# Two-layer decoder trunk on one core: a shorter run of plain units behind a block of seven products, and scratch transfers begun by GpSimd

## The chip, the cores and the metric

The kernel runs on one core of a Trainium2 chip. The metric is the device time of one execution in microseconds. Before the change it is 2709.37 us, the median of 3 runs (2709.22 to 2713.18).

TensorE multiplies matrices and writes its sums to PSUM; VectorE, ScalarE and GpSimd work on tiles in SBUF (the first two in PSUM too); SyncE begins DMA transfers. Each engine takes its instructions in the order in which the program gives them, and waits for the others by semaphores.

## The reference, cut to what matters

Two layers work on a residual stream `x` of 256 tokens by 2048 features, all in float32:

```python
for i in range(2):
    h = rms_norm(x, mix_norm[i])
    y = stick_breaking_mixer(h, ...) if i == 0 else gated_deltanet_mixer(h, ...)
    x = x + y
    x = x + (silu(g) * u) @ w_down[i]     # g, u = split(rms_norm(x, ffn_norm[i]) @ w_gu[i])
```

The first mixer projects to q, k and v (2048 x 6144), normalises q and k per head, takes q k^T for 16 heads of 128, weights each past key by a stick-breaking product, multiplies with v and projects out (2048 x 2048). The second is a gated DeltaNet (GDN) with a 2048 x 12352 input projection, a short convolution, a chunked recurrence and a 4096 x 2048 output projection. Each FFN has a hidden width of 5632: `w_gu` is 2048 x 11264 and `w_down` 5632 x 2048.

## The kernel before, in words

**Units.** All weights go through the core once. A *block* is a product of the 256 tokens with 512 columns of a weight; it is cut into *units* of 256 rows of it (512 KB). A unit is loaded by SyncE (`load`, L519), split by ScalarE into a rounded high part (L328) and by VectorE into the low rest (L332) (`convert`), and multiplied by TensorE (`product`, L354): high by high, high by low and low by high. A plain unit is 12 matmuls of 512 columns.

**Blocks of seven products.** In each FFN the gate and up columns of the hidden parts 0, 2, 4, 6, 8 and 10 (`SEVEN`), 12 blocks in all, are computed by a scheme of the Strassen kind: 7 products of half-size blocks in place of 8, 21 matmuls of 256 columns to a unit. It needs sums of the weights' quarters (`sums`, on VectorE, three instructions) and of the operands'. A block has eight units. At its end `quarters` reads out the four PSUM banks with one ScalarE and four VectorE instructions, and the next such block may begin only then. Seven-product units have two buffers of converted weights ("w" in the rows), plain units among them two others ("slabs").

**The order.** In an FFN, ten plain units in the ordinary lane come first, then a part in which seven-product and plain units are mixed, then plain ones. `merge` (L1026) chooses the mix by a search over all orders with a list of penalties: 4 for each plain unit short of two behind a finished block, 1 more where there are just two, 0.3 for two seven-product units in a row (three are not allowed), 2 for more than three plain ones in a row, and 0.15 for each unit by which the plain ones depart by more than 1.5 from 1.3 (`RATIO`) per seven-product unit. Of equal orders the one found first stays.

**The planner.** The kernel writes its instructions in an order that a small clock model in Python sets. Blocks' ends, norms and attention heads are tasks (generators); `stream` goes through the units, converts up to three units ahead (`AHEAD`), gives a unit's products and lets tasks run between them (`tick`). A task that has yielded goes on when the model's time for its last instructions has passed. A transfer's end is modelled by `transfer`; `later` and `nap` add pauses before a task's next step. The model only sets the order; on the chip the semaphores hold.

**Scratch transfers.** Some 128 x 1024 tiles are transposed by way of DRAM: VectorE transposes 32 x 32 pieces in place (L897 and L939), four writes of 32 partitions put them in place in a scratch tile (`way`, 128 KB each in runs of 128 bytes), and two reads bring them back in runs of 512 bytes (256 KB each). `turn` (L891) does this for q and k of the attention layer (8 sets) and for six parts of the norms' inputs; `turned_pairs` (L933) does it for the FFN's hidden activations (11 sets to each FFN), which it then splits into high and low operands ("kh", "kl") for the down projection. All these transfers are begun by SyncE at L367, in one queue with the weight loads. `turn` and `turned_pairs` pause before the first write (`TURN`, `WAY`) and between writes (`STEP`, `NAP`). GpSimd only fills tiles with constants, in the GDN layer above all.

Of the kernel before, what the change touches and what calls it, by code (L numbers as in the profile page):

```python
# [15 lines left out]
P = 128  # L16
D = 2048
S = 256
NT = S // P
# [12 lines left out]
class Slots:  # L32
# [37 lines left out]
    def put(self, *items):  # L70
        self.free.extend(items)
# [86 lines left out]
class Trunk:  # L158
# [20 lines left out]
    CONST = 14.0  # L179
    EARLY = 6  # L180
    LATER = 1.5
    WAY, NAP = 3.0, 1.2
    TURN, STEP = 1.0, 1.2
    TURNED = ((1, 0), (1, 1), (2, 0), (2, 1), (3, 0), (3, 1))
    GDN_ORDER = [('qk', 0), ('ba',), ('v', 0), ('qk', 1), ('z', 0), ('v', 2), ('v', 1), ('z', 1), ('qk', 2), ('qk', 3), ('v', 3), ('z', 2), ('z', 3), ('out', 0, 4), ('out', 4, 8), ('qk', 4), ('v', 4), ('qk', 5), ('v', 5), ('z', 5), ('z', 4), ('qk', 7), ('v', 6), ('qk', 6), ('out', 8, 16), ('v', 7), ('z', 6), ('z', 7), ('out', 16, 24), ('out', 24, 32)]

# [179 lines left out]
    def dma(self, out, in_):  # L366
        self.nc.sync.dma_start(out, in_)  # L367
        n = 4
        for d in out.shape:
            n *= d  # L370
        self.cur.ends("dma", self.transfer(n * (2 if out.shape[-1] * 4 <= 512 else 1), self.cur.begins("dma")))

    def transfer(self, nbytes, ready):
        issue = max(self.t["sp"], ready, self.t["pe"])
        self.t["sp"] = issue + 0.46
        self.t["dma"] = max(self.t["dma"], issue + 1.55) + nbytes / 3.6e5
        return self.t["dma"] + 0.55
# [367 lines left out]
    def norm_part(self, st, n):  # L745

        turned = (st.k, n) in self.TURNED
        if turned:
            parts = yield from self.two()
            yield from self.turn(parts, src=[self.x[t][n] for t in range(NT)])  # L750
        for half in range(2):
            if turned:
                src, put = parts[half], self.slabs.put
            else:
                src, put = (yield from self.banks.get()), self.banks.put
            bv = src.rearrange("p (k s) -> p k s", k=2)
            if not turned:
                for j in range(2):
                    kk = half * 2 + j
                    for t in range(NT):  # L760
                        self.tr(bv[:, j, t * P:(t + 1) * P], self.x[t][n][:, kk * P:(kk + 1) * P])
                yield
            kts = [n * 4 + half * 2 + j for j in range(2)]
            ops = [st.ops[kt] for kt in kts]
            gains = [self.gains[:, st.gain0 + kt:st.gain0 + kt + 1] for kt in kts]
            for j, o in enumerate(ops):
                self.act(o.hi, bv[:, j, :], scale=gains[j])
            for j, o in enumerate(ops):
                self.stt(o.lo, bv[:, j, :], gains[j], o.hi.bitcast(F32), ALU.mult, ALU.subtract)
                o.ready = True  # L770
            if st.forms is None:
                put(src)
            else:
                task = self.spawn(self.form_sums(st, n * 2 + half, src, put), f"forms {n} {half}")
                task.ready = self.t["pe"] + 2.0
        task = self.spawn(self.norm_stats(st, n), f"stats {n}")
        task.ready = self.t["pe"] + self.REST
# [110 lines left out]
        b = yield from self.slabs.get()  # L888
        return [a, b]

    def turn(self, parts, back=False, src=None):  # L891

        way = yield from self.ways.get()
        for i, s in enumerate(parts):
            self.nc.vector.transpose(s, src[i] if src else s)  # L897
            self.spend("dve", 0.07 + 0.00104 * NB)
            self.weave()
        self.cur.later = self.TURN  # L900
        yield
        flat = way[:]
        both = parts[0].tensor is parts[1].tensor and parts[1].offset - parts[0].offset == NB
        apart = not back and not both

        rows = (flat.rearrange("(c t) j -> c (t j)", t=2) if apart else flat).rearrange("(b i) j -> i b j", i=32)
        k = 0
        for a in range(4):
            m = slice(32 * a, 32 * a + 32)
            for n in range(1 if both else 2):  # L910
                if both:
                    dst, at = rows[:, :, m], self.joined(parts[0], 2)[m, :]
                elif back:
                    dst, at = rows[:, 16 * n:16 * n + 16, m], parts[n][m, :]
                else:
                    dst, at = rows[:, :, n * P + 32 * a:n * P + 32 * a + 32], parts[n][m, :]
                self.dma(dst, at.rearrange("p (b j) -> p b j", j=32))
                k += 1
            self.cur.nap = self.STEP if a < 3 else None
            yield  # L920
        for n in range(2):
            if back:
                self.dma(parts[n].rearrange("p (k c) -> p k c", k=4), flat.rearrange("(k t p) c -> t p k c", t=NT, p=P)[n])
            elif apart:
                self.dma(parts[n].rearrange("p (k c) -> p k c", k=2),
                         flat.rearrange("(c t) j -> c (t j)", t=2)[S * n:S * n + S, :].rearrange("(k p) c -> p k c", p=P))
            else:
                self.dma(self.joined(parts[0], 2).rearrange("p (k s) -> p k s", k=4)[:, :, n * P:(n + 1) * P],
                         flat[n * NB:(n + 1) * NB, :].rearrange("(k p) s -> p k s", p=P))
        yield  # L930
        self.ways.put(way)

    def turned_pairs(self, tok, stage, ops, put):  # L933

        way = yield from self.ways.get()
        for s, t in zip(self.cut(stage, NB), self.cut(tok, NB)):
            self.nc.vector.transpose(s, t)  # L939
            self.spend("dve", 0.07 + 0.00104 * NB)  # L940
            self.weave()
        self.cur.later = self.WAY
        yield

        rows = way[:].rearrange("(b i) j -> i b j", i=32)
        for a in range(4):
            m = slice(32 * a, 32 * a + 32)
            self.dma(rows[:, :, m], stage[m, :].rearrange("p (b j) -> p b j", j=32))
            self.cur.nap = self.NAP if a < 3 else None
            yield  # L950
        for t in range(NT):
            self.dma(tok.rearrange("p (k s) -> p k s", k=4)[:, :, t * P:(t + 1) * P],
                     way[t * NB:(t + 1) * NB, :].rearrange("(k p) s -> p k s", p=P))
            self.cur.nap = self.NAP if t < NT - 1 else None
            yield
        self.ways.put(way)
        if stage is not tok:
            self.duos.put(stage)
        for n, l in enumerate(self.cut(tok, NB)):
            pair = yield from self.pairs.get()  # L960
            self.operands_of(ops[2 * n:2 * n + 2], pair, l.rearrange("p (k s) -> p k s", k=2))
        put()


    def ffn_units(self, layer, norm, nxt, last, before, ahead=0):
# [52 lines left out]
        for b, n in zip(mids, turn):  # L1018
            b.sets = (n,)
# [6 lines left out]
    def merge(self, s, o):  # L1026


        ns, no = len(s), len(o)
        ends = [u.last for u in s]  # L1030
        best = {(0, 0, 0, 1, 3): (0.0, None)}
        layer = best
        trail = []
        for _ in range(ns + no):
            nextl = {}
            for st, (cost, _p) in layer.items():
                i, j, kind, run, gs = st

                for k in (0, 1):
                    ii, jj = i + k, j + 1 - k  # L1040
                    if ii > ns or jj > no or (k and kind == 1 and run >= 2):
                        continue
                    c = cost
                    if k:
                        c += 4.0 * max(0, 2 - gs) + (1.0 if gs == 2 else 0)
                        c += 0.3 * (kind == 1)
                        g2 = 0 if ends[i] else 3
                    else:
                        g2 = min(3, gs + 1)
                    r = min(run + 1, 4) if k == kind else 1  # L1050
                    if not k and r > 3 and ii < ns:
                        c += 2.0
                    if ii < ns:
                        c += 0.15 * max(0.0, abs(jj - self.RATIO * ii) - 1.5)
                    key = (ii, jj, k, r, g2)
                    if key not in nextl or nextl[key][0] > c:
                        nextl[key] = (c, st)
            trail.append(nextl)
            layer = nextl
        st = min(layer, key=lambda q: layer[q][0])  # L1060
        order = []
        for nextl in reversed(trail):
            order.append(st[2])
            st = nextl[st][1]
        return order[::-1]
# [727 lines left out]
```

## Time and profile before

| what | value |
|---|---|
| median of 3 runs | 2709.37 us |
| profiled execution | 2705.98 us |
| its span, first to last instruction | 2704.3 us |
| TensorE busy | 2669.4 us (99%) |
| VectorE busy | 2182.7 us (81%) |
| ScalarE busy | 1491.8 us (55%) |
| GpSimd busy | 11.2 us |
| granted TensorE clock | 1.0 |
| scratch writes, reads | 144, 72 |

In the profile PE is TensorE's matmuls, PEld its weight loads, DVE VectorE, ACT ScalarE, POOL GpSimd and SP SyncE; "SPq" means that SyncE's queue is meant. A row of the timeline has the start in us from the span's start, the length in us, the engine, the line of the kernel, the operation, the tiles written and read, how often, and in brackets the engine's idle time before it with what ended it. A row of the waits has who waited for whom, the total in us, how often, and the longest. Matmuls overlap, so the length of one (0.39 us for 512 columns) is more than the distance to the next (0.227 us).

### The profile page before, as it was taken

The numbers are of one execution on the slowest core, as the hardware profiler recorded it, in microseconds if no ns is written. First come the engines' busy times: TensorE is split into PE (matmuls) and PEld (weight loads), VectorE is DVE, ScalarE is ACT, GpSimd is POOL, SyncE is SP. The second block draws the span as 40 slices with busy tenths as digits, with TensorE's granted clock in tenths as the row PEclk, the third lists the DMA queues.
The fourth block names the chain that finished last, engine by engine and source line by source line (L and its number), as shares of the span: only waits on it lengthen the run. The fifth ranks groups of instructions, "written<-read, shape, count | busy, mean of one in ns | idle before, by whom it ended". The sixth has DMA issues, their size and how long they took to land.

```text
span 2704.3 us, 39527 instructions
## 1 busy us (share of the span) xinstructions
PE 2669.4 (99%) x14730; PEld 2274.6 (84%) x14730; DVE 2182.7 (81%) x3451; ACT 1491.8 (55%) x1961; POOL 11.2 (0%) x95
## 2 busy tenths in 40 slices
PE   9999999999999999999999999999999999999999
PEld 7888888888888888888888888888878888888887
DVE  6556568899999897678778887887679899989885
ACT  6555556554555554565665556645575555555453
POOL 0000000000000000000000000000000000000000
PEclk9999999999999999999999999999999999999999
DMA  7766775787676777855656556556567767767776
GB/s 245 202 185 196 219 211 164 208 231 212 203 218 205 208 211 233 227 174 172 182 143 195 159 161 175 168 153 186 170 191 212 223 196 220 217 188 218 226 209 188
DMA packets 487611, 534.41 MB, mean 198 GB/s; under 512 B 188087, under 2 KB 267258, under 8 KB 487418
## 3 DMA queue, kind: packets, MB, share of 16 engines
q1 hardware_dynamic: 487370, 531.87, 67.1%
q8 instruction: 115, 1.88, 0.3%
q14 instruction: 78, 0.64, 0.1%
q10 hardware_dynamic: 48, 0.02, 0.0%
HBM read 508.20 MB, written 23.59 MB: 197 GB/s over the span
## 4 chain that ended last, share of the span: by engine, by line
PE 83%; DVE 10%; issue 2%; ACT 2%; DMA 2%; SPq 0%; ACTq 0%; DVEq 0%
PE acc L354 61%; PE bank L354 20%; DVE w L332 5%; DVE slabs L332 2%; PE bank L363 1%; DMA slab<-in_ffn_w_gu_dram 1%; ACT slabs L328 1%; ACT w L328 1%; DVE slab L338 1%; DVE slab L332 1%; DVE slab L939 1%; DMA slab<-in_ffn_w_down_dram 0%; ACT slab L328 0%; DVE x L332 0%; DMA w<-in_ffn_w_gu_dram 0%
## 5 line engine op out<-in xcount | busy, mean ns | idle before, releaser
L332 DVE TENSOR_TENSOR w<-w,w 128x1024 fp32r<-128x1024 f32 (+2 forms) x746 | 946.3, 1285 | 249.0 <-ACT w L328 247.6
L328 ACT ACTIVATE w<-w 128x1024 fp32r<-128x1024 f32 (+2 forms) x650 | 802.8, 1244 | 417.8 <-PE acc L354 347.0
L354 PE MATMUL acc<-w,hTh 128*128 128x512 f32 (+1 forms) x3232 | 925.0, 369 | 9.1 <-DVE w L332 8.4
L354 PEld LDWEIGHTS acc<-w,hTh 128*128 128x128 f32 x3232 | 585.9, 189 | 120.5 <-DVE w L332 14.5
L354 PE MATMUL acc<-w,hTl 128*128 128x512 f32 (+1 forms) x1616 | 590.2, 365 | 3.1 <-DVE hTl L338 3.1
L328 ACT ACTIVATE slabs<-slab 128x1024 fp32r<-128x1024 f32 x264 | 279.3, 1058 | 431.9 <-DMA slab<-in_ffn_w_gu_dram 123.8
L332 DVE TENSOR_TENSOR slabs<-slab,slabs 128x1024 fp32r<-128x1024 f32 x264 | 321.5, 1218 | 93.1 <-ACT slabs L328 93.1
L354 PE MATMUL acc<-w,kh 128*128 128x512 f32 x1184 | 369.6, 393 | 0.0
L354 PEld LDWEIGHTS acc<-w,hTl 128*128 128x128 f32 x1616 | 304.5, 188 | 53.5 <-DVE hTl L338 3.9
L332 DVE TENSOR_TENSOR w<-w 128x256 f32<-128x256 f32 (+1 forms) x576 | 291.2, 508 | 9.8 <-DMA w<-in_ffn_w_gu_dram 2.6
L354 PEld LDWEIGHTS acc<-w,kh 128*128 128x128 f32 x1184 | 218.8, 188 | 43.7
L354 PE MATMUL acc<-w,kl 128*128 128x512 f32 x592 | 230.7, 390 | 0.0
L354 PE MATMUL acc<-slabs,hTh 128*128 128x512 f32 x608 | 190.1, 392 | 2.8 <-DVE slabs L332 2.8
L354 PE MATMUL bank<-w,wide 128*128 128x256 f32 x1296 | 178.9, 283 | 0.0
L354 PEld LDWEIGHTS bank<-w,wide 128*128 128x128 f32 x1296 | 165.8, 192 | 0.0
L354 PE MATMUL bank<-slabs,hTh 128*128 128x512 f32 x512 | 159.9, 392 | 3.1 <-DVE slabs L332 3.1
L354 PE MATMUL bank<-slabs,kh 128*128 128x512 f32 x512 | 159.6, 392 | 3.4 <-DVE slabs L332 3.4
L354 PE MATMUL acc<-slabs,kh 128*128 128x512 f32 x480 | 149.9, 392 | 2.1 <-DVE slabs L332 1.9
L354 PEld LDWEIGHTS acc<-slabs,hTh 128*128 128x128 f32 x608 | 111.0, 188 | 25.1 <-DVE slabs L332 4.9
L354 PEld LDWEIGHTS acc<-w,kl 128*128 128x128 f32 x592 | 111.1, 188 | 23.4
L354 PE MATMUL acc<-slabs,hTl 128*128 128x512 f32 x304 | 118.3, 389 | 0.0
L328 ACT ACTIVATE slab<-bank 32x128 f32<-32x128 f32 (+4 forms) x181 | 67.9, 379 | 89.3 <-PE bank L354 87.1
(216 smaller groups left out, 2933.4 us busy)
## 6 DMA issues: line engine op xcount, KB each, us to landing
w<-in_ffn_w_gu_dram SPq DMA_DIRECT2D x212, 512.0 KB, 4.5
slab<-in_ffn_w_gu_dram SPq DMA_DIRECT2D x140, 512.0 KB, 4.5
w<-in_gdn_w_in_dram SPq DMA_DIRECT2D x129, 512.0 KB, 4.3
slab<-in_ffn_w_down_dram SPq DMA_DIRECT2D x124, 512.0 KB, 4.5
w<-in_sb_w_in_dram SPq DMA_DIRECT2D x96, 512.0 KB, 4.5
w<-in_gdn_w_in_dram SPq DMA_DIRECT2D x128, 256.0 KB, 3.7
w<-in_gdn_w_out_dram SPq DMA_DIRECT2D x64, 512.0 KB, 4.4
w<-in_ffn_w_down_dram SPq DMA_DIRECT2D x52, 512.0 KB, 5.5
```

The lines of the kernel that those rows point to most:

```text
L328: self.nc.scalar.activation(out, in_, func, **kw)
L332: self.nc.vector.tensor_tensor(out, a, b, op=op)
L338: self.nc.vector.scalar_tensor_tensor(out, a, s, b, op0=op0, op1=op1)
L354: self.nc.tensor.matmul(out, lhsT, rhs, start=start, stop=stop, skip_group_check=True)
L363: self.nc.tensor.transpose(out, in_, self.ident[:p, :p])
L939: self.nc.vector.transpose(s, t)
```

## The change

The penalty of 1 for just two plain units behind a block of seven products is dropped. The scratch transfers of `turned_pairs`, and of `turn` for q and k, are begun by GpSimd through a new function `way_dma`; those of the norms stay with SyncE, with the pauses that they had (`LATE`, `NEXT`). In the model a transfer begun by GpSimd takes 6.5 us from its beginning (`OWN`), and takes no time of SyncE's queue or of the modelled DMA; the pauses before and between them are shorter.

```diff
-    WAY, NAP = 3.0, 1.2
-    TURN, STEP = 1.0, 1.2
+    WAY, NAP = 0.5, 0.8
+    TURN, STEP = 0.3, 0.8
+    OWN = 6.5
+    LATE, NEXT = 1.0, 1.2
...
+    def way_dma(self, out, in_):
+
+        self.nc.gpsimd.dma_start(out, in_)
+        self.cur.ends("dma", max(self.cur.begins("dma"), self.t["pe"]) + self.OWN)
...
-            yield from self.turn(parts, src=[self.x[t][n] for t in range(NT)])
+            yield from self.turn(parts, src=[self.x[t][n] for t in range(NT)], sp=True)
...
-    def turn(self, parts, back=False, src=None):
+    def turn(self, parts, back=False, src=None, sp=False):
...
         way = yield from self.ways.get()
+        move = self.dma if sp else self.way_dma
...
-        self.cur.later = self.TURN
+        self.cur.later = self.LATE if sp else self.TURN
...
-                self.dma(dst, at.rearrange("p (b j) -> p b j", j=32))
+                move(dst, at.rearrange("p (b j) -> p b j", j=32))
                 k += 1
-            self.cur.nap = self.STEP if a < 3 else None
+            self.cur.nap = (self.NEXT if sp else self.STEP) if a < 3 else None
...
-                self.dma(self.joined(parts[0], 2).rearrange("p (k s) -> p k s", k=4)[:, :, n * P:(n + 1) * P],
+                move(self.joined(parts[0], 2).rearrange("p (k s) -> p k s", k=4)[:, :, n * P:(n + 1) * P],
...
-            self.dma(rows[:, :, m], stage[m, :].rearrange("p (b j) -> p b j", j=32))
+            self.way_dma(rows[:, :, m], stage[m, :].rearrange("p (b j) -> p b j", j=32))
...
-            self.dma(tok.rearrange("p (k s) -> p k s", k=4)[:, :, t * P:(t + 1) * P],
+            self.way_dma(tok.rearrange("p (k s) -> p k s", k=4)[:, :, t * P:(t + 1) * P],
...
-                        c += 4.0 * max(0, 2 - gs) + (1.0 if gs == 2 else 0)
+                        c += 4.0 * max(0, 2 - gs)
```

More of the change, by code (lines that the diff above doesn't have):

```diff
@@ L922, in turn @@
             if back:
-                self.dma(parts[n].rearrange("p (k c) -> p k c", k=4), flat.rearrange("(k t p) c -> t p k c", t=NT, p=P)[n])
+                move(parts[n].rearrange("p (k c) -> p k c", k=4), flat.rearrange("(k t p) c -> t p k c", t=NT, p=P)[n])
             elif apart:
-                self.dma(parts[n].rearrange("p (k c) -> p k c", k=2),
+                move(parts[n].rearrange("p (k c) -> p k c", k=2),
                          flat.rearrange("(c t) j -> c (t j)", t=2)[S * n:S * n + S, :].rearrange("(k p) c -> p k c", p=P))
             else:
-                self.dma(self.joined(parts[0], 2).rearrange("p (k s) -> p k s", k=4)[:, :, n * P:(n + 1) * P],
+                move(self.joined(parts[0], 2).rearrange("p (k s) -> p k s", k=4)[:, :, n * P:(n + 1) * P],
                          flat[n * NB:(n + 1) * NB, :].rearrange("(k p) s -> p k s", p=P))
```

## The prediction

> **What bounds the kernel now.** I read the page's busy shares and its chain of waits first, then the stage table, then TensorE's waits.
>
> ```profile
> PE 2669.4 (99%) x14730; PEld 2274.6 (84%) x14730; DVE 2182.7 (81%) x3451; ACT 1491.8 (55%) x1961; POOL 11.2 (0%) x95
> PE 83%; DVE 10%; issue 2%; ACT 2%; DMA 2%; SPq 0%; ACTq 0%; DVEq 0%
> ```
>
> TensorE sets the time; its work isn't changed. All that a change of order can win is its idle time, 2704.3 - 2669.4 = 34.9 us. The stage table (start and length of the stretch, then PE, PEld, DVE, ACT busy) shows where that lies.
>
> ```profile
> 0.00:405.00 405.00, 398.16 (x1813) 330.25 (x1814) 244.10 (x317) 225.61 (x332) 2.70 (x14) 1.00 0.72 210
> 485.00:1040.00 555.00, 546.98 (x3261) 485.45 (x3260) 505.73 (x641) 292.79 (x255) 0.00 (x0) 1.00 0.72 211
> 2066.00:2620.00 554.00, 545.36 (x3248) 483.60 (x3248) 504.68 (x639) 292.69 (x255) 0.00 (x0) 1.00 0.72 210
> ```
>
> The first stretch is the attention layer, whose idle 6.8 us are nearly all start-up. The other two are the mixed parts of the FFNs, where units of seven products alternate with plain ones: 555.0 - 547.0 = 8.0 and 554.0 - 545.4 = 8.6 us idle, with VectorE at 91%. TensorE's waits say for whom:
>
> ```profile
> PE acc L354 <- DVE w L332: 8.4, 16, 1.0
> PE bank L354 <- DVE slabs L332: 6.5, 5, 1.6
> PE acc L354 <- DVE slabs L332: 4.7, 9, 0.9
> ```
>
> So it waits for converted weights: "slabs" are those of plain units, "w" those of seven-product units and of the unmixed stretches. It never waits for a weight transfer there; VectorE comes last. The timeline of one block end, on TensorE and then VectorE:
>
> ```profile
> 533.85 0.63 PE L354 MATMUL bank<-slabs,hTh 128*128 128x512 f32 x2
> ...
> 541.28 0.50 PE L354 MATMUL bank<-slabs,hTh 128*128 128x512 f32 x1 [1.57 <-DVE slabs L332]
> ```
>
> ```profile
> 532.63 1.23 DVE L332 TENSOR_TENSOR slabs<-slab,slabs 128x1024 fp32r<-128x1024 f32 x1 [3.15 <-ACT slabs L328]
> ...
> 538.83 1.29 DVE L939 STREAM_TRANSPOSE slab<-slab 128x512 f32<-128x512 f32 x2
> 540.04 1.18 DVE L332 TENSOR_TENSOR slabs<-slab,slabs 128x1024 fp32r<-128x1024 f32 x1
> 541.15 2.01 DVE L332 TENSOR_TENSOR w<-w,w 128x1792 fp32r<-128x1792 f32 x1
> ```
>
> The seven-product block ends at 533.85; three plain units follow, 2.72 us each (533.85, 536.6, 539.3 as they start). The wait of 1.57 us stands just inside the third. Plain units in the mix have two buffers of converted weights, so the third can't be converted before the first has run; by then VectorE is busy with reading out the ended block, and the third's conversion (540.04) stands behind that and behind the transposes. Before, VectorE had idled 3.15 us.
>
> **The change, the order of units.** The planner's list now takes two plain units behind a block at no penalty. Counting by hand: a block has eight seven-product units, seven gaps between them, and the list wants 1.3 x 8 = 10.4 plain units to a block. With three at the end, 7 + 3 = 10 fit and every second block has one double inside. With two and three equally cheap, ties go to the list that puts plain units early (they are tried first and a later equal one doesn't replace), so doubles go inside, one or two to a block, and two stay at the end. Units and products are the same in number.
>
> Removed: the waits in the third unit. Over both FFNs they are
>
> ```profile
> 491.89 0.50 PE L354 MATMUL acc<-slabs,hTh 128*128 128x512 f32 x1 [0.33 <-DVE slabs L332]
> 693.25 0.50 PE L354 MATMUL bank<-slabs,kh 128*128 128x512 f32 x1 [1.57 <-DVE slabs L332]
> 2072.48 0.50 PE L354 MATMUL acc<-slabs,hTh 128*128 128x512 f32 x1 [0.68 <-DVE slabs L332]
> 2121.87 0.50 PE L354 MATMUL bank<-slabs,hTh 128*128 128x512 f32 x1 [1.57 <-DVE slabs L332]
> 2172.92 0.50 PE L354 MATMUL bank<-slabs,kh 128*128 128x512 f32 x1 [0.23 <-DVE slabs L332]
> 2274.38 0.50 PE L354 MATMUL bank<-slabs,kh 128*128 128x512 f32 x1 [1.57 <-DVE slabs L332]
> ```
>
> With 541.28: 0.33 + 1.57 + 1.57 + 0.68 + 1.57 + 0.23 + 1.57 = 7.5 us, 45% of the two stages' 16.6.
>
> Added: the next block's first seven-product unit comes one plain unit earlier, with less cover. A block end without a wait shows its slack:
>
> ```profile
> 590.41 1.21 DVE L332 TENSOR_TENSOR slabs<-slab,slabs 128x1024 fp32r<-128x1024 f32 x1
> 591.88 2.02 DVE L332 TENSOR_TENSOR w<-w,w 128x1792 fp32r<-128x1792 f32 x1 [0.27 <-ACT w L328]
> 593.82 1.28 DVE L332 TENSOR_TENSOR x<-acc,x 128x512 f32<-128x512 f32 x2
> ```
>
> ```profile
> 586.25 0.63 PE L354 MATMUL acc<-slabs,kh 128*128 128x512 f32 x2
> ...
> 594.43 0.40 PE L354 MATMUL acc<-w,hTh 128*128 128x256 f32 x2
> ```
>
> The block ends at 586.25, the conversion at 593.82, the unit starts at 594.43: 0.6 us to spare. With two, it is due at 586.25 + 2 x 2.72 = 591.7. If the conversion stays where it is in VectorE's order, it loses only the third plain unit's 1.2 us and ends at 592.6: 0.9 us late. But the loop converts up to three units ahead before it lets the ended block's task run, so the conversion now goes ahead of the read-out, into time like the 3.15 us above, and the read-out has until 591.7. So a block end costs between 0 and 0.9 us; there are 2 x 11 with a block behind them, 0 to 20 us. I take 0.1, near the low end since the order of the loop decides it: +2.
>
> **The change, the scratch transfers.** 120 writes and 60 reads move from SyncE's queue to GpSimd's (of the 144 and 72 below, the norms' six sets of 4 and 2 stay).
>
> ```profile
> way<-slab SPq DMA_DIRECT2D x144, 128.0 KB, 5.3
> slab<-way SPq DMA_DIRECT2D x72, 256.0 KB, 5.0
> SPq L367 <- DMA way<-slab: 19.5, 12, 4.2
> ACT kh L328 <- DMA slab<-way: 25.2, 14, 5.0
> ```
>
> SyncE no longer stands 19.5 us in reads that wait for their writes, with weight loads behind. That is worth little: no TensorE wait in the mixed stages is ended by a transfer; an earlier load can only shorten VectorE's lateness behind it. I take -1, between 0 and a tenth of those 19.5, -2, since TensorE idles only 16.6 of the two stages' 1109 us. ScalarE's 25.2 us of waiting for landed reads holds up conversions behind it, but no TensorE wait follows from it: 0 now. The planner counts a set as landed 17.0 us after it begins (0.5 + 3 x 0.8 + 6.65 + 0.8 + 6.65) where it counted about 14.5, so the operands' conversions are placed later and ScalarE should wait less, also off the path. GpSimd itself is free (11.2 us busy); its reads now stand before the next set's writes, which nothing else queues behind until the GDN layer's fills.
>
> What no row shows is how long GpSimd takes to begin a write of 1024 runs of 128 bytes. The nearest is SyncE's own, in the tightest place, a k projection of the attention layer:
>
> ```profile
> 65.64 1.30 DVE L897 STREAM_TRANSPOSE slab<-slab 128x512 f32<-128x512 f32 x2
> 68.49 0.46 SPq L367 DMA_DIRECT2D way<-slab  x1
> 69.63 3.00 SPq L367 DMA_DIRECT2D way<-slab  x2
> 78.94 0.92 SPq L367 DMA_DIRECT2D slab<-way  x2
> DMA to landing us min/median/max: 3.9/4.4/4.9
> 84.94 0.81 PE L354 MATMUL bank<-slab 128*128 128x256 f32 x4
> ```
>
> The third of these writes holds SyncE 2.5 us, so a run of them goes at 1.2 to 1.5 us each. Transposed by 66.9, landed by about 83.5, used at 84.94, when the v projection's products are over: 1.4 us to spare. On GpSimd, with G us to begin a write and half of that a read (half as many runs), the k operand lands at 66.9 + 4G + 4.4 + G + 4.4, about 75.7 + 5G. Up to G = 1.8 nothing is late; above that TensorE stands 5 us for each us of G, in each of four head groups. Bounds: G = 0.46 (a lone issue) to 3.0 (SyncE's longest stretch for two), so 0 to 6 us x 4 = 24. I take G below 1.8 and 0, as SyncE's sustained rate is the nearest row.
>
> By the Trainium skill's DMA: Bandwidth & Descriptors, section Anatomy of one DMA — SWDGE (gpsimd) path, a transfer begun by GpSimd takes about 2.0 us and its bytes at 436 GB/s, 2.3 us for these writes, and many descriptors add little: an estimate by which k lands well before 84.94 and this term is 0. No run here shows it.
>
> **Sum.** 2705.98 (profiled execution; span 2704.3) - 7.5 + 2 - 1 = 2699.5. The median shown is 2709.37, 3.4 above that execution, so 2702.9; I say 2703.
>
> **Rivals.**
>
> First, the wait only changes place: the first seven-product unit, or the conversions behind it, take back what the third plain unit loses. VectorE's 91% speaks for it; the 3.15 us of idle VectorE ahead of the block end speaks against. Then -7.5 + 7 - 1: about 2708, no change.
>
> Second, two plain units are too few at every end: conversion behind read-out, 22 x 0.9 = 20 us: 2709.4 - 7.5 + 20 - 1 = 2721. It decides from 0.35 us an end. For it stands the 0.6 us of slack at 594.43; against it the loop's order.
>
> Third, GpSimd begins these writes slowly. At G = 3 each head group waits 75.7 + 15 - 84.9 = 5.8 us, 23 in all: 2703 + 23 = 2726; at G = 4, 2746. It decides from G = 2.1. For it: no such transfer is in the trace, and runs of 128 bytes already hold SyncE. A cause could be VectorE itself:
>
> ```profile
> L332 DVE TENSOR_TENSOR slabs<-slab,slabs 128x1024 fp32r<-128x1024 f32 x264 | 321.5, 1218 | 93.1 <-ACT slabs L328 93.1
> L897 DVE STREAM_TRANSPOSE slab<-slab 128x512 f32<-128x512 f32 x16 | 10.4, 687 | 0.0
> ```
>
> If VectorE held GpSimd off while it works, the sets would wait for its gaps, 161 us in the first 405; but these run at 1218 / 1024 = 1.19 and 687 / 512 = 1.34 ns an element, so none goes at a doubled rate. The Trainium skill's SBUF — State Buffer, section SBUF: two separate sides, warns against this very move: GpSimd can't write descriptors while VectorE runs in a two-port mode. By that rule the 1.19 ns rows are not such a mode and the trap stays open only for a handful of copies; no run here shows the lock.
>
> Fourth, the change does more than its terms: a better-filled VectorE clears most of the 16.6 us, 2709.4 - 14 = 2695. The other 16.6 - 7.5 = 9.1 us aren't behind a block's end, where the order gives way, so it has little.
>
> **How the numbers follow.** This measurement can tell about 0.2%, 5.4 us, from no change. My forecast (2703, own range 2699 to 2704) 0.36 and the fourth 0.07 make faster 0.43. The first, 0.28, is within. The second, 0.15, and the third, 0.14, are slower: 0.29. The range 2694 to 2727 leaves out most of the third above and a little of the fourth below.
>
> **What would show it.** Right: no TensorE wait two units behind a block's end, two plain units there; the idle time of the mixed stages at about 13 us together, not 16.6; ScalarE's wait for landed reads under 25 us; scratch writes on GpSimd about 1.5 us apart; the k operand landed before 84.9. Wrong: "PE <- DVE w" well above 8.4 us (second rival), TensorE waits for scratch reads in the attention layer (third), or the third unit's waits back at doubles inside a block (first).

## The result, and the profile after

| | before | after |
|---|---|---|
| median | 2709.4 us | 2692.4 us |
| profiled execution | 2705.98 us | 2691.59 us |
| its span | 2704.3 us | 2689.9 us |

The changed kernel takes 0.9935 of the time of the one before, interval 0.992 to 0.995: 17 us less, where 6 were forecast, and just below the forecast's range of 2694 to 2727. Of the 17, 14.4 lie between the two profiled executions; the remaining 2.6 come from how each of these stands to its own median.

First the page's busy shares and the chain of waits of the kernel after:

```profile
PE 2665.0 (99%) x14730; PEld 2275.6 (85%) x14730; DVE 2186.8 (81%) x3451; ACT 1488.5 (55%) x1961; POOL 150.8 (6%) x275
PE 84%; DVE 11%; DMA 2%; issue 2%; ACT 2%; DVEq 0%; ACTq 0%
```

The chain is TensorE's as before (84% after 83%). Its idle time went from 34.9 to 24.9 us, its busy time from 2669.4 to 2665.0 with the same 14730 matmuls. I take the 4.4 us of "busy" for waits too: matmuls overlap, so a wait between two of them partly disappears in the modelled length of the one before. Below, waits are therefore also measured from start to start: the distance from one matmul's start to the next, less what this distance usually is for the shape (the 20th percentile of the same execution), counted from 0.1 us on.

The stretches that the prediction used (start and length, then PE, PEld, DVE, ACT busy) are now

```profile
0.00:405.00 405.00, 398.28 (x1819) 330.97 (x1820) 245.02 (x321) 226.09 (x336) 40.02 (x62) 1.00 0.68 211
485.00:1040.00 555.00, 551.00 (x3279) 489.97 (x3278) 510.34 (x645) 293.58 (x257) 41.84 (x54) 1.00 0.67 213
2066.00:2620.00 554.00, 551.01 (x3281) 490.84 (x3281) 511.78 (x645) 294.64 (x258) 44.98 (x58) 1.00 0.68 215
```

In the two mixed parts 4.0 and 3.0 us are idle, 7.0 where there were 16.6. The clock granted is 1.0 in both kernels. TensorE's waits after, rows for VectorE in the FFNs:

```profile
PE acc L356 <- DVE w L334: 7.7, 14, 1.0
...
PE bank L356 <- DVE slab L334: 2.0, 3, 0.8
...
PE bank L356 <- DVE slabs L334: 0.3, 1, 0.3
```

Waits for "slabs", the plain units' converted weights, fell from 6.5 + 4.7 = 11.2 us to 0.3. What is new is "bank <- DVE slab", 2.0 us: the first seven-product unit of a block stands until the read-out has emptied a bank. From start to start, over both mixed parts:

| waits of TensorE, us | before | after |
|---|---|---|
| third plain unit behind a block's end | 9.8 | 0 |
| plain units behind the first and second seven-product unit of a block | 6.2 | 0.7 |
| seven-product units | 14.8 | 17.1 |
| of these, the first one behind a block's end | 0 | 3.5 |
| sum | 30.8 | 17.8 |

That is 13.0 of the 14.4 us; the mixed parts are 5.1 and 8.0 us shorter. Another 1.2 us are gone by the start of the first mixed part; when the same kernel was profiled again (e8 below) they were 0.4, so this part isn't shown to be a gain.

The order is as counted by hand: all 11 ends with a block behind them have two plain units in each FFN, where all 11 had three, and blocks have one or two doubles, most of them early. The end that the prediction showed, in the timeline of after (TensorE, then VectorE):

```profile
535.40 0.63 PE L356 MATMUL bank<-slabs,hTh 128*128 128x512 f32 x2
...
540.87 0.40 PE L356 MATMUL acc<-w,hTh 128*128 128x256 f32 x2
```

```profile
534.18 1.23 DVE L334 TENSOR_TENSOR slabs<-slab,slabs 128x1024 fp32r<-128x1024 f32 x1 [0.98 <-ACT slabs L330]
...
536.12 2.02 DVE L334 TENSOR_TENSOR w<-w,w 128x1792 fp32r<-128x1792 f32 x1
538.05 0.68 DVE L334 TENSOR_TENSOR slab<-acc,slab 128x512 f32<-128x512 f32 x1
538.77 1.74 DVE L334 TENSOR_TENSOR slab<-bank,slab 128x512 f32<-128x512 f32 x3
...
541.03 1.22 DVE L334 TENSOR_TENSOR slabs<-slab,slabs 128x1024 fp32r<-128x1024 f32 x1
```

The block ends at 535.40. The next seven-product unit's conversion (536.12) goes ahead of the read-out (538.05 to 540.51), as the prediction read the loop. The plain conversion that stood behind the read-out and made TensorE wait (540.04 before) now serves a plain unit behind the seven-product one. The price is the margin: the read-out is over 0.4 us before the unit starts at 540.87.

The scratch transfers, from the groups of GpSimd, the DMA queues and the DMA issues (the last figure of an issue's row is the median time to landing):

```profile
L377 POOL DMA_DIRECT2D way<-slab x120 | 94.2, 792 | 1522.9 <-DVE slab L947 864.1 <-DVE w L334 287.2 <-DVE slab L905 207.6
L377 POOL DMA_DIRECT2D slab<-way x60 | 45.4, 761 | 169.3 <-DMA way<-slab 142.4 <-PE acc L356 11.8 <-PE bank L356 5.5
```

```profile
q1 hardware_dynamic: 330890, 500.40, 59.6%
q0 software_dynamic: 10560, 31.47, 4.2%
...
way<-slab POOLq DMA_DIRECT2D x120, 128.0 KB, 5.0
slab<-way POOLq DMA_DIRECT2D x60, 256.0 KB, 4.6
```

GpSimd begins a write in 0.79 us and a read in 0.76. ScalarE's wait for landed reads ("kh <- DMA slab<-way", 25.2 us before) is 0.2 us.

### The profile page after: what moved, and what is told of

Same layout as the page of the kernel before. It is cut to its first block, busy times and chain, and to the rows that moved or that the text cites. A ratio compares the mean times of both kernels' runs of the same rounds, so it can differ in the third digit from the quotient of the medians.

```text
span 2689.9 us, 39694 instructions
## 1 busy us (share of the span) xinstructions
PE 2665.0 (99%) x14730; PEld 2275.6 (85%) x14730; DVE 2186.8 (81%) x3451; ACT 1488.5 (55%) x1961; POOL 150.8 (6%) x275
## 2 busy tenths in 40 slices
DMA packets 341692, 534.41 MB, mean 199 GB/s; under 512 B 65207, under 2 KB 113658, under 8 KB 341498
## 3 DMA queue, kind: packets, MB, share of 16 engines
q1 hardware_dynamic: 330890, 500.40, 59.6%
q0 software_dynamic: 10560, 31.47, 4.2%
## 4 chain that ended last, share of the span: by engine, by line
PE 84%; DVE 11%; DMA 2%; issue 2%; ACT 2%; DVEq 0%; ACTq 0%
PE acc L356 61%; PE bank L356 22%; DVE w L334 5%; DVE slabs L334 3%; PE bank L365 1%; DMA slab<-in_ffn_w_down_dram 1%; DVE slab L334 1%; ACT slabs L330 1%; DVE x L334 1%; ACT w L330 1%; DMA slab<-in_ffn_w_gu_dram 0%; DVE slab L340 0%; DVE slab L947 0%; DVE hTl L340 0%; DMA x<-in_x_dram 0%
## 5 line engine op out<-in xcount | busy, mean ns | idle before, releaser
L334 DVE TENSOR_TENSOR w<-w 128x256 f32<-128x256 f32 (+1 forms) x576 | 292.3, 508 | 12.2 <-DMA w<-in_ffn_w_gu_dram 4.1
L377 POOL DMA_DIRECT2D way<-slab x120 | 94.2, 792 | 1522.9 <-DVE slab L947 864.1
```

The lines of the kernel that those rows point to most:

```text
L334: self.nc.vector.tensor_tensor(out, a, b, op=op)
L377: self.nc.gpsimd.dma_start(out, in_)
```

## The experiments

Ratios are to the kernel before; each has its 95% interval. "Alone" edits are made to the kernel before.

| kernel | median us | ratio | interval |
|---|---|---|---|
| after | 2692.4 | 0.9935 | 0.992 to 0.995 |
| e1 order alone | 2697.2 | 0.9952 | 0.994 to 0.9965 |
| e2 transfers and model alone | 2709.4 | 0.9997 | 0.9989 to 1.0006 |
| e3 GpSimd's queue alone | 2707.7 | 0.9997 | 0.9988 to 1.0006 |
| e4 after, by SyncE | 2698.4 | 0.9957 | 0.9944 to 0.997 |
| e5 two at the ends, doubles late | 2713.8 | 1.0017 | 1.0008 to 1.0026 |
| e6 one at the ends | 2713.9 | 1.0013 | 1.0004 to 1.0022 |
| e7 read-out later | 2740.6 | 1.0116 | 1.0102 to 1.0129 |
| e8 after, again | 2691.4 | 0.9936 | 0.9923 to 0.9948 |
| e9 order alone, shifted | 2698.7 | 0.9962 | 0.995 to 0.9975 |
| e10 before, shifted | 2711.1 | 1.0008 | 0.9999 to 1.0017 |
| e11 after, shifted to 2 | 2697.2 | 0.9953 | 0.9939 to 0.9966 |
| e12 after, shifted to 4 | 2688.7 | 0.9930 | 0.9917 to 0.9942 |
| e13 by SyncE, converted later | 2695.8 | 0.9945 | 0.9933 to 0.9958 |
| e14 after, converted earlier | 2701.9 | 0.9971 | 0.9961 to 0.9982 |
| e15 order and GpSimd's queue | 2693.7 | 0.9949 | 0.9935 to 0.9962 |

And TensorE's waits in the mixed parts, from start to start, by where they stand in the block (us, both FFNs of one profiled execution). Column P8 is the plain units behind the eighth seven-product unit, that is, behind the end; P1-2 those behind the first and second; P3-7 the rest. P8 also holds the plain units just ahead of the first block. S1 is a block's first seven-product unit, S2-8 the others. One execution scatters: after and e8 are the same kernel, and their seven-product units wait 17.1 and 13.8 us.

| kernel | P8 | P1-2 | P3-7 | S1 | S2-8 |
|---|---|---|---|---|---|
| before | 9.8 | 6.2 | 0 | 2.5 | 12.4 |
| after | 0 | 0.7 | 0 | 6.0 | 11.2 |
| e1 order alone | 0.2 | 0.3 | 0 | 7.8 | 12.8 |
| e3 queue alone | 7.7 | 6.0 | 0.3 | 2.5 | 12.0 |
| e5 late doubles | 0 | 3.8 | 8.5 | 10.3 | 10.7 |
| e6 one at the ends | 0 | 1.3 | 0 | 26.8 | 5.5 |
| e7 read-out later | 2.0 | 7.2 | 0.3 | 34.6 | 14.6 |
| e9 order, shifted | 1.9 | 2.8 | 1.1 | 7.5 | 3.8 |
| e10 before, shifted | 23.7 | 3.1 | 0.3 | 0.4 | 8.1 |
| e15 order and queue | 0 | 0 | 0 | 2.5 | 10.5 |

### Which half of the change: e1, e2

e1 is the kernel before without the penalty:

```diff
-                        c += 4.0 * max(0, 2 - gs) + (1.0 if gs == 2 else 0)
+                        c += 4.0 * max(0, 2 - gs)
```

> Only the penalty for two plain units behind a block is dropped; every transfer stays with SyncE and the planner's pauses are those of before. Theory O (the gain is the order of the units: the waits of the third plain unit and those that followed from them): 10 to 14 us under before, about 2697, with the two mixed stages 4 to 8 us shorter each. Rival Q (the gain is the queue: SyncE and the transfer engines are relieved): within 4 us of before. Rival B (both are needed, because a shorter cover at the block's end only works when weights come earlier): slower than before by some us.

e2 is the changed kernel with that line as it was before.

> The other half alone: scratch transfers by GpSimd with the new pauses and the longer latency in the planner, but the old penalty, so three plain units behind a block. Theory O: 1 to 4 us under before, the third unit's waits of 1.57 us still there. Rival Q: 10 to 14 us under before. Rival B: 0 to 3 us under before.

Measured: 12 us less for the order alone, nothing for the transfers and their model alone (theory O expected 1 to 4 us). So most of the gain is the order's. But the two don't add up by themselves: after is 5 us below e1 (the intervals just overlap).

### Taking the transfers apart: e3, e4

e3 is the kernel before, its model and order unchanged, with only the engine changed that begins the scratch transfers of `turned_pairs` and of q and k:

```diff
-    def dma(self, out, in_):
-        self.nc.sync.dma_start(out, in_)
+    def dma(self, out, in_, eng=None):
+        (eng or self.nc.sync).dma_start(out, in_)
...
-            self.dma(rows[:, :, m], stage[m, :].rearrange("p (b j) -> p b j", j=32))
+            self.dma(rows[:, :, m], stage[m, :].rearrange("p (b j) -> p b j", j=32), self.nc.gpsimd)
```

> The same transfers are begun by GpSimd, but the planner's model is that of before to the last figure, so all engines' instructions stand in the order of before and only the queue differs. Theory O: within 3 us of before, the same TensorE waits at the same places. Rival Q: 8 us or more under before. If the longer latency in the model is what makes GpSimd's transfers bearable, this kernel waits for landed scratch reads and is slower than the second of these kernels.

e4 is the changed kernel, order and model, with the transfers begun by SyncE:

```diff
-        self.nc.gpsimd.dma_start(out, in_)
+        self.nc.sync.dma_start(out, in_)
```

> The changed kernel with its planner and order untouched, but its scratch transfers begun by SyncE again: only the queue differs from the changed kernel. Theory O: within 4 us of the changed kernel (2688 to 2697). Rivals Q and B: most of the gain is gone, 2703 or more.

With the old order the queue is worth nothing, although ScalarE's 25.2 us of waiting are gone in e3 as well: no TensorE wait followed from them. With the new order, SyncE's transfers give 2698, as in e1. That is just outside theory O's range, which ended at 2697, and far below the 2703 of its rivals.

### Why three plain units cost time: e5, e6, e7

e5 is e1 with ties decided for the other order, so that most doubles stand later in a block:

```diff
-                for k in (0, 1):
+                for k in (1, 0):
```

> The first of these kernels (two plain units behind a block, transfers with SyncE) with ties of the search broken the other way, so that the doubles inside a block stand late in it instead of early. Theory P (the place that matters is the block's end: three in a row there is what costs): 10 to 14 us under before, as with early doubles (2697). Rival D (early doubles give VectorE the slack that the read-out behind a block's end needs): 2703 or more, with TensorE's waits inside seven-product units longer.

TensorE's waits in e5, the rows for banks and plain units:

```profile
PE bank L354 <- DVE slab L332: 3.2, 4, 0.8
PE bank L354 <- DVE x L332: 2.1, 2, 1.1
PE acc L354 <- ACT slabs L328: 2.0, 2, 1.1
PE bank L354 <- DVE slabs L332: 2.0, 5, 0.9
```

Two plain units at every end, and no gain. The table by place says where it went: P8 is 0, as in e1, but the plain units behind the second, third, fourth and sixth seven-product unit wait 12.3 us, where e1 has 0.3. The waits inside seven-product units, which rival D named as its sign, aren't longer (21.0 us against 20.6).

The 12.3 us have more than one cause. Some 4.8 us, behind second and third units, are waits for conversions that VectorE came to late, with no idle time in the 7 us and more before them. Here it is in arrears behind the read-out. An early double gives it 2.72 us of TensorE's time for one more conversion of 1.2 us, in which arrears can be worked off; without one they go on through the block. Another 4.6 us stand behind the sixth unit of the third block, and there VectorE had been idle. SyncE, ScalarE, VectorE and TensorE in the first FFN:

```profile
568.05 1.68 SPq L519 DMA_DIRECT2D slab<-in_ffn_w_down_dram  x1
574.13 1.06 ACT L328 ACTIVATE slabs<-slab 128x1024 fp32r<-128x1024 f32 x1 [3.92 <-DMA slab<-in_ffn_w_down_dram]
575.22 1.23 DVE L332 TENSOR_TENSOR slabs<-slab,slabs 128x1024 fp32r<-128x1024 f32 x1 [1.78 <-ACT slabs L328]
575.24 0.49 PE L354 MATMUL acc<-slabs,kh 128*128 128x512 f32 x1 [0.94 <-ACT slabs L328]
```

A weight load came late; SyncE had begun it behind two scratch writes. In the second FFN the same load, begun at 2151.67, landed at 2157.97, and ScalarE took it at 2158.07. And 2.6 us, behind the fourth unit of the fourth block, are waits for a PSUM bank whose sums VectorE had not yet added to x at a plain block's end (the row "bank <- DVE x"). Whether late doubles brought these two about, or only how the loads and the plain blocks' ends happen to fall, isn't shown: e5 wasn't run shifted as the others are below. So two units at the end don't bring the gain by themselves; that the unit's new place just behind the read-out does is shown for 4.8 of the 12.3 us.

e6 is e1 with one plain unit allowed behind an end:

```diff
-                        c += 4.0 * max(0, 2 - gs)
+                        c += 4.0 * max(0, 1 - gs)
```

> One plain unit behind a block is free of penalty, so that most blocks end with one and hold one more double inside. The prediction's second rival (too short a cover behind the end, conversion behind read-out) must bite here if it bites anywhere: the read-out takes about 4.5 us from the block's end and one plain unit covers 2.7, so each end should cost 1 to 2 us in the first seven-product unit, 20 to 40 us in all, 2715 or more. If waits do not grow so, the cover is not what matters and the kernel stays at 2690 to 2700.

```profile
PE bank L354 <- DVE slab L332: 11.3, 16, 1.0
PE acc L354 <- DVE slab L332: 6.5, 6, 2.3
```

Now the read-out isn't over when the next block begins: S1 goes from 7.8 to 26.8 us, and the time is just under the 2715 expected at least. This is the second rival's mechanism, at one plain unit instead of two, and by the read-out instead of the conversion.

e7 is the kernel before with the read-out given 2.8 us later, so that the third plain unit's conversion goes ahead of it:

```diff
     def quarters(self, acc, free):
...
+        self.cur.later = 2.8
+        yield
```

> The order of units and the transfers are those of before; only the task that reads out a block of seven products begins 2.8 us later in the planner, so that the third plain unit's conversion stands ahead of the read-out in VectorE's order. If the third unit waits because its conversion stands behind the read-out, its waits (9.8 us over both mixed stages, counted from one matmul's start to the next) fall below 3 us; what the later read-out then costs shows in the first seven-product unit behind it. Net -6 to +3 us. If the third unit waits for something else (its load, ScalarE, the buffer alone), its waits stay at 8 us or more.

```profile
PE bank L354 <- DVE slab L332: 17.6, 22, 0.8
...
PE acc L354 <- DVE slab L332: 5.2, 6, 1.1
```

P8 falls from 9.8 to 2.0: the third unit did wait because its conversion stood behind the read-out. But S1 rises by 32 us, and the kernel loses 31 us where a change of -6 to +3 was expected. Both pieces of work fit between the end and the next block only if one of them isn't there.

### Is it the place or the coincidence: e8 to e12

e8 is the changed kernel once more.

> The changed kernel itself, in the same job as the others. If the queue adds nothing to the order, it is at 2696 to 2699 like the order alone (2697.15) and the same order with SyncE (2698.41); if the transfers add 4 to 6 us on top of the order, as the first measurement of it suggests, it is at 2691 to 2694.

The plain units are themselves blocks whose ends need VectorE, and they fall somewhere against the seven-product blocks' ends. Moving all plain units by one against these tells whether the gain is such a coincidence. e9 is e1, e10 the kernel before, e12 the changed kernel with

```diff
-    BEFORE = 3
+    BEFORE = 4
```

and e11 the changed kernel with `BEFORE = 2`.

> The kernel before with the penalty of 1 dropped, and 4 plain units instead of 3 ahead of the mixed part (BEFORE), so that every plain block's end and every k-slice of it falls one unit elsewhere against the blocks of seven products. If the gain of the order comes from where the plain units stand (two behind an end, a double soon after), it stays: 2697 us, within 4. If it came from how the plain blocks' ends happen to fall against the ends of the seven-product blocks, it isn't kept: 2704 to 2712 us.

> The kernel before with nothing but 4 plain units instead of 3 ahead of the mixed part: three plain units stay behind every end. If the places set the time: 2709 us, within 4, and 12 us above the same shift with the changed order. If the coincidence of the blocks' ends sets it, this one has the same chance to gain: it lies within 4 us of the shifted changed order, on either side.

> The changed kernel with 2 plain units instead of 3 ahead of the mixed part. If the places set the time: 2692 us, within 4. If the coincidence of the ends does: 2698 to 2708 us.

> The changed kernel with 4 plain units instead of 3 ahead of the mixed part. If the places set the time: 2692 us, within 4, and 3 to 7 us below the shifted changed order with SyncE's transfers (what GpSimd's transfers are worth on top of the order, a second look at it). If the coincidence of the ends does: 2698 to 2708 us. If GpSimd's transfers are worth nothing on top of the order: no more than 2 us below that kernel.

The two orders stay 12.4 us apart when shifted, as they were 12.2 unshifted. In e10 the third unit's waits even grow, to 19.4 of the 23.7 us under P8; TensorE's rows for plain units are

```profile
PE bank L354 <- DVE slabs L332: 8.9, 7, 1.8
PE acc L354 <- DVE slabs L332: 7.4, 13, 3.0
```

So the places set the gain; the coincidence moves the time by some 5 us on top (2688.7, 2692.4 and 2697.2 for 4, 3 and 2, where e11 missed what was expected of it). e12 has the lowest median, 2688.7 us, but its interval overlaps that of after, so no better version is shown. On e9, e12 gains 10 us, more than expected of the transfers, and here the intervals are apart.

### What the transfers are worth on top of the order: e13, e14, e15

Two causes were open: ScalarE's waits for landed reads, and SyncE's queue. e13 is e4 with `OWN = 9.0` in place of 6.5, e14 the changed kernel with `OWN = 4.0`.

> The changed kernel with its scratch transfers begun by SyncE, and the model's latency 9.0 us instead of 6.5, so that ScalarE is given the operands' conversions about 5 us later in the order and its 48.9 us of waits for landed reads go mostly away. If those waits cost the 5 us: 2692 us, within 3, as the changed kernel. If SyncE's queue costs them: 2698 us, within 3, as without the longer latency. If the 5 us are no more than the scatter from one order of the conversions to another, either is possible, and the next run won't answer in kind.

> The changed kernel (GpSimd's transfers) with the model's latency 4.0 us instead of 6.5: ScalarE is given the conversions about 5 us earlier and waits some 40 us for landed reads again. If those waits cost the 5 us: 2697 us, within 3. If SyncE's queue cost them: 2692 us, within 3.

ScalarE's waits moved the way that was meant, in e14 to 24.4 us where some 40 were expected. In e4, e13 and e14, in this order:

```profile
ACT kh L330 <- DMA slab<-way: 48.9, 20, 5.4
```

```profile
ACT kh L330 <- DMA slab<-way: 6.5, 9, 1.7
```

```profile
ACT kh L330 <- DMA slab<-way: 24.4, 14, 3.0
```

e13 came out at 2695.8, between the two answers: within 3 us of "SyncE's queue" (2698), 3.8 from "the waits" (2692), with an interval that holds 2698 and overlaps that of after. e14 was slower than both, but not by these waits: its mixed parts are as long as after's (592.8 + 587.9 against 591.1 + 589.1 us). It lost 8.6 us in the attention layer, where the shorter latency also moved k's transfers. TensorE's wait there, and one such place in the timelines of GpSimd and TensorE:

```profile
PE bank L356 <- DMA slab<-way: 3.6, 4, 1.5
```

```profile
72.39 3.14 POOL L377 DMA_DIRECT2D way<-slab  x4 [15.87 <-DVE slab L905]
82.11 1.51 POOL L377 DMA_DIRECT2D slab<-way  x2 [6.58 <-DMA way<-slab]
```

```profile
85.94 0.67 PE L356 MATMUL bank<-slab 128*128 128x256 f32 x2 [1.23 <-issue]
88.11 0.80 PE L356 MATMUL bank<-slab 128*128 128x128 f32 x2 [1.51 <-DMA slab<-way]
```

The reads begin at 82.1 and q k^T at 85.9: TensorE stands at each of the four head groups. In the changed kernel the reads begin at 75.2 and the operand is used at 86.5.

e15 is e3 with the penalty dropped: the new order and GpSimd's queue under the old model.

> The kernel before with the penalty of 1 dropped and the scratch transfers, the norms' apart, begun by GpSimd; the model keeps its latencies and pauses for them, and its picture of SyncE's queue. If GpSimd's queue by itself brings the 5 us: 2692 us, within 3. If they need the model's longer latency as well: 2697 us, within 3.

2693.7 us is nearer to the answer "queue alone", but its interval overlaps e1's. Its profiled execution differs from e1's mainly in one place: S1 is 2.5 instead of 7.8 us, and the first unit behind an end doesn't wait at all (5.3 us in e1). The two executions are extremes, though: e1's is the slowest of its five (2699.99), e15's the fastest of its five (2691.69), so they lie 8.3 us apart where the medians lie 3.4 apart, and how much of the 5.3 is the queue's isn't shown. One end in both kernels, e1 first: SyncE's load of a plain unit's weights, ScalarE's and VectorE's conversion of them, the read-out, TensorE.

```profile
729.18 0.37 SPq L519 DMA_DIRECT2D slab<-in_ffn_w_down_dram  x1
...
735.38 1.06 ACT L328 ACTIVATE slabs<-slab 128x1024 fp32r<-128x1024 f32 x1 [6.28 <-DMA slab<-in_ffn_w_down_dram]
...
736.47 1.22 DVE L332 TENSOR_TENSOR slabs<-slab,slabs 128x1024 fp32r<-128x1024 f32 x1 [2.66 <-ACT slabs L328]
...
741.79 1.75 DVE L332 TENSOR_TENSOR slab<-bank,slab 128x512 f32<-128x512 f32 x3
...
743.26 0.50 PE L354 MATMUL bank<-w,hTh 128*128 128x256 f32 x2 [0.83 <-DVE slab L332]
```

```profile
726.49 0.37 SPq L519 DMA_DIRECT2D slab<-in_ffn_w_down_dram  x1
...
730.83 1.06 ACT L328 ACTIVATE slabs<-slab 128x1024 fp32r<-128x1024 f32 x1 [4.72 <-DMA slab<-in_ffn_w_down_dram]
...
731.92 1.23 DVE L332 TENSOR_TENSOR slabs<-slab,slabs 128x1024 fp32r<-128x1024 f32 x1 [0.80 <-ACT slabs L328]
...
737.24 1.75 DVE L332 TENSOR_TENSOR slab<-bank,slab 128x512 f32<-128x512 f32 x3
...
738.75 0.47 PE L354 MATMUL bank<-w,hTh 128*128 128x256 f32 x2
```

From the load's issue to ScalarE's start 6.2 us go by in e1 and 4.3 in e15. VectorE idles 2.66 us for it instead of 0.80, and the read-out ends just too late. Over the kernel ScalarE's waits for the gate and up weights of plain units, e1 and then e15, are

```profile
ACT slabs L328 <- DMA slab<-in_ffn_w_gu_dram: 139.4, 61, 6.0
```

```profile
ACT slabs L328 <- DMA slab<-in_ffn_w_gu_dram: 86.0, 42, 5.8
```

By themselves these two say little: in after and e8, the same kernel, this wait is 81.2 and 114.1 us. With the waits for the down weights added, it is 227 us in e1, 213 in e4 and 197 before, and with GpSimd's queue 176 in e15, 171 in after, 172 in e8 and 163 in e3. So with GpSimd's queue ScalarE waits less for loads, under either order; and the place above shows how, with the new order, a late weight load can reach TensorE by way of VectorE's read-out. Why this very load took 1.9 us longer isn't shown: no scratch transfer was begun in the 12 us before it.

## Why the prediction was wrong, point by point

**What bounds the kernel.** Right: TensorE's work didn't change, and the gain lies in waits for VectorE in the mixed parts.

**The order.** Right in each count: two plain units at every end, one or two doubles inside, early ones by the tie. That the tie mattered this much (e5) wasn't seen.

**The removed waits, -7.5 us: the step that failed.** The third unit's waits went, but the sum was too small in two ways. Its rows show idle time alone; from start to start the same waits are 9.8 us. And the sentence "The other 16.6 - 7.5 = 9.1 us aren't behind a block's end, where the order gives way, so it has little" was wrong. 6.2 us from start to start lay in the plain units behind the first and second seven-product unit. They all stand behind the end of an up block (the second of a pair of gate and up), where VectorE, after the read-out, has still the product of gate and up to do and its transposes, and often a plain block's end. One such place before, on VectorE and then TensorE (the block ended at 834.7):

```profile
842.24 1.28 DVE L332 TENSOR_TENSOR x<-bank,x 128x512 f32<-128x512 f32 x2
843.44 1.41 DVE L338 SCALAR_TENSOR_TENSOR slab<-slab,rstd 128x512 f32<-128x512 f32 x2
...
845.37 1.22 DVE L332 TENSOR_TENSOR slabs<-slab,slabs 128x1024 fp32r<-128x1024 f32 x1
```

```profile
846.64 0.50 PE L354 MATMUL acc<-slabs,kh 128*128 128x512 f32 x1 [0.88 <-DVE slabs L332]
```

For 4.1 of the 6.2 us the order had changed right there, because the third unit went there as a double; the other 2.0, in the fifth block of each FFN, went without a new double at that place. So the step took a block's end to be over with the third unit, where VectorE's lateness lasts into the next block. The term measured 15.98 - 0.68 = 15.3 us; in e1, with the order alone, it is 15.98 - 0.56 = 15.4. With late doubles (e5) 12.3 us of waits at plain units come back, 4.8 of them by this lateness.

**The added wait, +2 us, and the transfers, -1.** Taken one by one, both were off, and they hang together. With SyncE's transfers (e1) seven-product units wait 20.6 us, 5.8 more than before; with GpSimd's 17.1 in after, 13.8 in e8 and 13.0 in e15, from 2.3 more to 1.8 less. With the new order and the new model, SyncE's transfers give 18.8 (e4) and 17.1 (e13), GpSimd's in e14 15.9. So with SyncE the shorter cover costs 2 to 6 us, and with GpSimd's queue between 2.3 us and nothing: the ranges touch, and each figure is of one execution. With the old order there was nothing to take back (e3: 14.5 against 14.8). The prediction counted what SyncE's relief was worth at the old order, "no TensorE wait in the mixed stages is ended by a transfer", and didn't ask again after taking the cover away. Measured on top of the order, the transfers with their model go with 4.8 us less (after against e1), and 10 shifted (e12 against e9); the queue alone with 3.4 (e15 against e1) and 6.0 (after against e4). Of these four only the shifted pair has intervals that lie apart. That GpSimd's transfers are worth something under the new order is shown by that pair; how it divides between late loads, ScalarE's waits for landed reads (e13: 2.6 us less without most of them, intervals overlapping) and the coincidence of ends stays open.

**The sum.** 2699.5 was worked out for a profiled execution that took 2691.59. By start to start the terms measured -15.3 + 2.3 in the mixed parts and -1.2 ahead of them, in this execution: 2705.98 - 14.2 = 2691.8. The last 2.6 us of the miss are the 3.4 that were added to come to a median: the changed kernel's median lies 0.8 above its profiled execution. Of the signs named, the idle time of the mixed parts was to be 13 us and is 7.0; the scratch writes were to stand 1.5 us apart and stand 0.79; ScalarE's landed-read waits went as foreseen. That the added wait came to 2.3 us where +2 was forecast is luck: e1 has 5.8, and the rest went with a relief that the prediction didn't foresee.

**The rivals.** The first (the wait changes place) is what e5, e6 and e7 do, not the change itself; there it cost 4 us or more, not nothing. The second was wrong at two plain units (TensorE's wait for "w" fell from 8.4 to 7.7 us, where it was to rise) and right at one: e6 loses 17 us on e1, near the 20 forecast, and the point from which it decides lies between one unit and two. The third is dead as it was put: G is 0.79 us, below the 1.8 from which it would count, and the k operand of the first group, due at 84.94, has its reads begun at 75.2 and 76.0 and landing in a median of 4.4 us. Its place is real, though: e14 lost 8.6 us there. The fourth, given 0.07, is what happened; its 2695 is 2.6 us above the median.

**GpSimd's descriptors.** GpSimd's time to begin a write is 784 to 932 ns in all 120, with VectorE busy for 81% of the span, so the lock that the Trainium skill's SBUF — State Buffer, section SBUF: two separate sides, warns of doesn't show. This is the side on which the prediction left it: VectorE's rows at 1.19 and 1.34 ns an element. The Trainium skill's DMA: Bandwidth & Descriptors, section Anatomy of one DMA — SWDGE (gpsimd) path, gives 2.3 us for one of these writes as an estimate; the trace's median to landing is 5.0, twice that, in the company of the weight loads. Its rule that many descriptors add little agrees with the trace: a write of 1024 runs takes 0.79 us to begin, a read with half as many 0.76.

## What to carry to other kernels

When an engine that several waits share is in arrears after one event, count all waits up to where the arrears are worked off, not only those at the event, and count them from start to start, since overlapping matmuls hide part of a wait in their length. Where a unit of cover stands matters as much as how many there are: two units at an end won 12 us with the doubles early in the block and nothing with them later, though less than half of the waits that came back are shown to be unpaid arrears. A relief that is worth nothing under one order has to be priced again under the other: the same transfers by GpSimd were worth nothing with the old order and, shifted, 10 us with the new one.

## What the runs showed of the hardware

GpSimd's time to begin a transfer hardly depends on the number of runs in the two forms here: 0.79 us for 1024 runs of 128 bytes, 0.76 for 512 runs of 512. SyncE, which the profile of before shows held 2.5 us by the third such write in a row, takes 0.37 us for most weight loads. The moved transfers also appear as fewer packets, 341692 instead of 487611 in all: 10560 on GpSimd's queue for 31.47 MB, 3 KB each. The share of the DMA engines fell from 67.1% to 59.6 + 4.2 = 63.8%. By itself this had no effect on the time (e3: 0.9997).
